# Block products for 16 of the 22 k tiles of the first FFN's down product

## Chip, cores and metric

The kernel runs on one core of a Trainium2 chip. The metric is the device time of one execution in microseconds. Three runs of the kernel before gave 1197.14, 1197.54 and 1198.35 us; the median is 1197.54.

## The reference

A transformer block on 512 tokens of width 1024 in fp32: an FFN, a mixer and a second FFN, each added to the residual x. The part that matters here is the first FFN.

```python
def swiglu(x, w_gu, w_down):
    g, u = jnp.split(x @ w_gu, 2, axis=-1)
    return (jax.nn.silu(g) * u) @ w_down
...
    for l in range(DEPTH):
        x = x + FFN_RES_WEIGHT * swiglu(rmsnorm(x, norm_ffn1_g[l]), ffn1_w_gu[l], ffn1_w_down[l])
        x = x + hybrid_mixer(rmsnorm(x, norm_mix_g[l]), w_in[l], ...)
        x = x + FFN_RES_WEIGHT * swiglu(rmsnorm(x, norm_ffn2_g[l]), ffn2_w_gu[l], ffn2_w_down[l])
```

FFN_RES_WEIGHT is 0.5 and the inner width D_FF is 2816, which is 22 k tiles of 128 (KF). The down product is 512 tokens x 2816 by 2816 x 1024.

## The kernel before

**Layout.** x and the hidden activations lie transposed: features on the 128 partitions, tokens along the free dimension. `hid` holds the 22 k tiles of the down product's input, each 128 x 512. X holds the residual, eight tiles of 128 x 512. Every fp32 factor is split into a rounded part h and a remainder l, and a product is three matmuls: h x h, h x l and l x h. For weights the two parts are the tiles `wh` (a cast on ScalarE, L335) and `wl` (a subtraction on VectorE, L336), in pools of three buffers each. For activations they are pairs of tiles `op`, 14 buffers in all.

**Plain k tiles.** One weight unit of 128 x 1024 is one k tile; `mm` multiplies it into eight PSUM banks, one for each of the eight output tiles d, with 3 x 8 = 24 matmuls of 512 columns (L363 to L365). [...]

**Sets.** A set computes 4 output tiles over 8 k tiles for all 512 tokens by seven block products in place of eight: k is halved into 4 + 4 tiles, the output columns into 256 + 256, the tokens into 256 + 256 (HW = 256), and sums of blocks are multiplied. The products are named m1, p2, q6, p5, q7, p4, p3. Each is 24 x matmul of 256 columns, written `Set.run` (L528), and is called a step below. The set's weights are four raw tiles a11, a12, a21, a22 of 128 x 1024. Their sums are made on the way: s3 = a11 + a21 on VectorE (L320), and a21 += a22, a11 += a21, a12 += a11 by accumulating transfers on POOL's queue (L310), each due before the product that uses it. m1, q6, q7 and p4 of a set accumulate in one bank, p2 in a second, p5 and p3 in a third. In the down product each product is added into X right after it (L741), so the bank must be read before the next of its products goes on in it.

**Operands.** The activation side of the seven products is an `Operands` object: seven parts, each a pair of `op` tiles. `make(p)` casts (ScalarE, L576) and subtracts (VectorE, L577); for p5, q6, q7 and p4 a sum in place on `hid` comes first (VectorE, L556 to L563). All sets over the same 8 k tiles share one such object, so one holds all 14 `op` buffers; a buffer comes free once the last set has used its part.

**Order.** `STEPS` lists units and products in the order in which TensorE takes them. `order` chains sets: the m1 and p2 of the next set stand among the last products of the present one. `Weights.issue` runs up to three steps ahead of TensorE: it loads raw tiles (SP's queue, L306, a pool `f` of 10 buffers), six steps ahead for a set, and converts them. A scheduler then sets each engine's order; every engine runs its queue in that order.

**The first FFN's down product** comes after a chain of nine up sets (the last is called the last up set below). The hidden tiles 8 to 19 are multiplied plainly (CHUNK = 8, TAIL1 = 2), and meanwhile the seven parts for tiles 0 to 7 are made. Two chained sets follow over tiles 0 to 7, one for each half of the output. Tiles 20 and 21 come last, plainly, since the last up set writes them; with them the next norm starts. The second FFN's down product (`last_down`) is another code path.

Of the kernel before, what the change touches and what calls it, by code (L numbers as in the profile page):

```python
# [17 lines left out]
D = 1024  # L18
KD = D // P
DFF = 2816  # L20
KF = DFF // P
# [19 lines left out]
TAIL = 4  # L41

TAIL1 = 2


def k_parts(kt):
# [3 lines left out]
def single(mat, kt, col):  # L50
    return [(mat, k0, nk, (col,), P) for k0, nk in k_parts(kt)]


def group(mat, kt, cols, slow=False):

    parts = [(0, 1), (1, 1)] if slow else [(0, 2)]
    parts += [(k0, 2) for k0 in range(2, kt, 2)]
    return [(mat, k0, nk, tuple(cols), P) for k0, nk in parts]
# [6 lines left out]
def full(mat, kt):  # L65
    return [(mat, k, 1, (0,), 1024) for k in range(kt)]
# [12 lines left out]
HW = 256  # L79


def order(firsts):


    seq = []
    n = len(firsts)
    for i, s in enumerate(firsts):
        if i == 0:
            seq += [(s, "m1"), (s, "p2")]
        seq += [(s, "q6"), (s, "p5"), (s, "q7")]  # L90
        if i + 1 < n:
            t = firsts[i + 1]
            seq += [(t, "m1"), (s, "p4")]
            seq += [(t, "p2"), (s, "p3")] if i + 2 < n else [(s, "p3")]
        else:
            seq += [(s, "p2"), (s, "p4"), (s, "p3")]
    return seq
# [6 lines left out]
PLAN = []  # L104
# [4 lines left out]
def units(us):  # L109
    for u in us:  # L110
        STEPS.append((len(PLAN), None))
        PLAN.append(u)


def sets(mat, pairs):
    firsts = []
    for cols in pairs:
        firsts.append(len(PLAN))
        PLAN.extend((mat, 4 * j, 4, (c,), HW) for c in cols for j in range(2))
    STEPS.extend(order(firsts))  # L120


# [7 lines left out]
CHUNK = 8  # L130
# [4 lines left out]
def last_plan(down):  # L135
    us = full(down, KF)
    units(us[CHUNK : KF - TAIL])
    firsts = []
    for s in range(2):
        firsts.append(len(PLAN))  # L140
        PLAN.extend((down, 4 * j + 2 * s, 2, (512 * i,), 512) for i in range(2) for j in range(2))
    CHUNK_STEP.update({(s, p): len(STEPS) + 2 * i + s for i, p in enumerate(CHUNK_ORDER)
                       for s in range(2)})
    STEPS.extend((n, p) for p in CHUNK_ORDER for n in firsts)
    units(us[KF - TAIL :])


def ffn_plan(up, down, plain, slow):

    units(group(up, KD, (0, DFF, P, DFF + P), slow))  # L150
    for f in range(2, plain):
        units(single(up, KD, f * P))
        units(single(up, KD, DFF + f * P))
    sets(up, [(s * HW, DFF + s * HW) for s in range(plain // 2, KF // 2)])
    if slow:
        us = full(down, KF)
        units(us[CHUNK : KF - TAIL1])
        sets(down, [(2 * s * HW, (2 * s + 1) * HW) for s in range(D // (2 * HW))])
        units(us[KF - TAIL1 :])
    else:  # L160
        last_plan(down)
    ENDS.append(len(STEPS))


def mixer_plan():
    units(group("w_in", KD, (QO, KO, QO + P, KO + P)))
    units(wide("w_in", KD, VO))
    for h in (2, 3):
        units(single("w_in", KD, QO + h * P))
        units(single("w_in", KD, KO + h * P))  # L170
    units(wide("w_in", KD, VO + 512))
    base = {"ga": GA, "gb": GB, "cb": CB, "r": RO}
    sets("w_in", [(CC + i * HW, CU + i * HW) if n == "conv" else
                  (base[n] + 2 * i * HW, base[n] + (2 * i + 1) * HW) for n, i in MSETS])
    for d in range(KD):
        units(single("w_out_conv", KD, d * P))
    for d in range(KD):
        units(single("w_out_gla", KD, d * P))
    units(group("w_o", KD, (0, P, 2 * P, 3 * P)))
    for d in range(4, KD):  # L180
        units(single("w_o", KD, d * P))
    ENDS.append(len(STEPS))
# [13 lines left out]
def block_kernel(ctx: ExitStack, tc: tile.TileContext, xT, vecs, gf, gup, wgl, wts, out):  # L196
# [5 lines left out]
    keep = ctx.enter_context(tc.tile_pool(name="keep", bufs=1))  # L202
    ps = ctx.enter_context(tc.tile_pool(name="ps", bufs=6, space=bass.MemoryType.PSUM))
# [14 lines left out]
    def tile_of(pool, shape, dtype=F32):  # L218
        cnt[0] += 1
        return pools[pool].tile(shape, dtype, tag=pool, name=f"{pool}{cnt[0]}")  # L220
# [141 lines left out]
    def mm3(o, wh, wl, ah, al, first, last):  # L362
        nc.tensor.matmul(o, wh, ah, start=first, stop=False)  # L363
        nc.tensor.matmul(o, wh, al, start=False, stop=False)  # L364
        nc.tensor.matmul(o, wl, ah, start=False, stop=last)  # L365
# [171 lines left out]
    class Operands:  # L537
# [29 lines left out]
        def make(self, p):  # L567
            if p in self.parts:
                return
            i = self.ORDER.index(p)  # L570
            if i > 0:
                self.make(self.ORDER[i - 1])
            v = self.sum(p)
            h, l = (tile_of("op", [P, 1024], F32R) for _ in range(2))
            hv, lv = (t.rearrange("p (k t) -> p k t", t=HW) for t in (h, l))
            nc.scalar.copy(hv, v)  # L576
            nc.vector.tensor_tensor(out=lv, in0=v, in1=hv.bitcast(F32), op=ALU.subtract)  # L577
            self.parts[p] = (h, l)
# [4 lines left out]
    def run_sets(make, ahead=2, hooks={}):  # L583


        at = W.taken
        seq = []
        while STEPS[at + len(seq)][1] is not None:
            seq.append(STEPS[at + len(seq)])
        sets = {n: None for n, _ in seq}  # L590
        number = {n: i for i, n in enumerate(sets)}
        for n, i in number.items():
            sets[n] = make(i)
        for i, (n, p) in enumerate(seq):
            for n_, p_ in seq[i : i + ahead + 1]:
                sets[n_].group.make(p_)
            sets[n].run(p)
            for f in hooks.get((number[n], p), ()):
                f()


    def ffn(up, down, norm, nxt, plain, at):
# [9 lines left out]
        hid = tile_of("hid", [P, KF, S])  # L612
# [69 lines left out]
        def pair(t):  # L682
            return t.rearrange("p (e t) -> p e t", t=HW)
# [3 lines left out]
        def split_hid(k):  # L687

            h, l = (tile_of("op", [P, 2, S], F32R) for _ in range(2))
            t = hid[:, k : k + 2]  # L690
            nc.scalar.copy(h, t)
            nc.vector.tensor_tensor(out=l, in0=t, in1=h.bitcast(F32), op=ALU.subtract)
            return h, l

        us = full(down, KF)
# [3 lines left out]
        def banks():  # L699
            return [AUX(), AUX()] + [MM() for _ in range(KD - 2)]  # L700

        def mm(d, k, w, hl):
            c = slice(d * P, (d + 1) * P)
            mm3(o[d], w[0][:, c], w[1][:, c], hl[0][:, k % 2], hl[1][:, k % 2],
                k in (CHUNK, KF - TAIL1), k in (KF - TAIL1 - 1, KF - 1))

        def add_half(d):
            nc.vector.scalar_tensor_tensor(out=x[d], in0=o[d], scalar=0.5, in1=x[d],
                                           op0=ALU.mult, op1=ALU.add)


        ho = Operands(lambda j, l: hid[:, 4 * j : 4 * j + 4, l * HW : (l + 1) * HW])
        o = banks()
        hls = {k: split_hid(k) for k in (CHUNK, CHUNK + 2)}
        more = [4, 6, 8, 10, "m1", "p2", "p5", "q6", "q7", "p3"]
        for k in range(CHUNK, KF - TAIL1):
            w = W.take(us[k])
            for d in range(KD):
                mm(d, k, w, hls[k - k % 2])
            if more:  # L720
                n = more.pop(0)
                if isinstance(n, int):
                    hls[CHUNK + n] = split_hid(CHUNK + n)
                else:
                    ho.make(n)
        for d in range(KD):
            add_half(d)
        ho.make("p4")

        X = XS[-1]  # L730

# [4 lines left out]
        def down_set(i):  # L736
            def done(s, p):
                for l, a, by in uses[p]:
                    xt = X[:, 4 * i + 2 * a : 4 * i + 2 * a + 2, l * HW : (l + 1) * HW]
                    bank = s.bank[{"p2": "a", "p5": "c", "p3": "c"}.get(p, "b")]  # L740
                    nc.vector.scalar_tensor_tensor(out=xt, in0=pair(bank), scalar=by, in1=xt,  # L741
                                                   op0=ALU.mult, op1=ALU.add)

            return Set(ho, done, keep=())

        run_sets(down_set)
        o = banks()
        w = [W.take(u) for u in us[KF - TAIL1 :]]
        hl = split_hid(KF - TAIL1)
        for d in range(KD):  # L750
            for i in range(TAIL1):
                mm(d, KF - TAIL1 + i, w[i], hl)
            add_half(d)
            nxt.add(d)
# [696 lines left out]
```

## Time and the profile before

| what | value |
|---|---|
| median of three runs | 1197.54 us (1197.14 to 1198.35) |
| profiled execution | its span, first to last instruction, is 1196.1 us; the page gives no other time for it, so its own device time is only known as about that of the runs, 1.4 us above the span at their median |
| mean granted TensorE clock | 0.998 |
| busy | PE 99%, PE weight load 92%, VectorE 69%, ScalarE 49%, POOL 8% |
| twelve plain down tiles | 232.20 to 297.51 us |
| two down sets | 297.51 to 337.82 us |

In the page's rows a group is: line, engine, operation, output <- input, count, busy time, mean duration, idle time ahead of it and what ended that. PE is matmuls, PEld weight loads, DVE VectorE, ACT ScalarE, POOL GpSimd and its queue, SP the queue of plain loads. A row of the windows gives each engine's busy time in a stretch and the count of its instructions, then the granted clock (1.00 is full) and what the transfers did. A row of the timeline gives start and duration.

### The profile page before, as it was taken

The page shows a single profiled execution, that of the slowest core. Times are in us where ns is not written, and L with a number is a line of the kernel's source. Part 1 is how long each engine was busy: PE and PEld are TensorE (multiplying, and loading weights), DVE is VectorE, ACT ScalarE, POOL GpSimd, SP SyncE. Part 2 cuts the span into 40 slices and gives each one's busy share as a digit, 9 for nine tenths or more (in the row PEclk, how much of TensorE's full clock was granted, in tenths as well). Part 3 has the DMA queues.
Part 4 walks back from the last instruction along what each step waited for, and adds up shares of the span by engine and source line. Part 5 has one row for each costly group of instructions (what it writes and reads, how often), then busy time and mean ns, then how long its engine had stood idle before and what let it go on. Part 6 is the DMA issues. An engine that isn't in the chain of part 4 may idle for free.

```text
span 1196.1 us, 19145 instructions
## 1 busy us (share of the span) xinstructions
PE 1188.1 (99%) x7858; PEld 1095.6 (92%) x7858; DVE 830.7 (69%) x997; ACT 587.3 (49%) x730; POOL 101.2 (8%) x137
## 2 busy tenths in 40 slices
PE   9999999999999999999999999999999999999997
PEld 8899999988988889999999998888889999998886
DVE  7976566844787765858678686555597656675685
ACT  6564444622354465646454574324355455562353
POOL 0011111000110001011011100100001111100100
PEclk9999999999999999999999999999999999999999
DMA  9377777533473225767767766613338777763431
GB/s 346 87 207 187 180 184 187 176 101 80 104 270 106 88 66 146 201 183 188 191 179 175 190 185 211 203 48 141 120 74 209 167 188 173 186 180 108 93 95 70
DMA packets 57607, 187.65 MB, mean 157 GB/s; under 512 B 6480, under 2 KB 10704, under 8 KB 57520
## 3 DMA queue, kind: packets, MB, share of 16 engines
q1 hardware_dynamic: 36912, 124.27, 29.5%
q0 software_dynamic: 15968, 57.68, 26.1%
q10 hardware_dynamic: 4640, 4.49, 1.2%
q8 instruction: 61, 1.00, 0.3%
q14 instruction: 26, 0.21, 0.1%
HBM read 124.55 MB, written 8.39 MB: 111 GB/s over the span
## 4 chain that ended last, share of the span: by engine, by line
PE 99%; ACT 0%; DVE 0%; issue 0%; POOL 0%; POOLq 0%
PE mm L528 54%; PE mm L387 7%; PE mm L363 6%; PE mm L365 6%; PE mm L364 6%; PE mm L829 3%; PE mm L779 2%; PE mm L780 2%; PE mm L778 2%; PE mm L405 1%; PE mm L406 1%; PE mm L404 1%; PE aux L1120 1%; PE aux L363 1%; PE aux L364 1%; PE aux L780 1%
## 5 line engine op out<-in xcount | busy, mean ns | idle before, releaser
L528 PE MATMUL mm<-op,wh 128*128 128x256 f32 x3584 | 648.0, 283 | 0.0
L335 ACT CAST wh<-f 128x1024 fp32r<-128x1024 f32 (+1 forms) x319 | 333.4, 1046 | 467.3 <-PE mm L528 235.3
L528 PEld LDWEIGHTS mm<-op,wh 128*128 128x128 f32 x3584 | 558.9, 192 | 1.0
L336 DVE TENSOR_TENSOR wl<-f,wh 128x1024 fp32r<-128x1024 f32 (+1 forms) x319 | 387.6, 1218 | 203.8 <-ACT wh L335 199.0
L528 PE MATMUL mm<-op,wl 128*128 128x256 f32 x1792 | 507.3, 283 | 0.0
L528 PEld LDWEIGHTS mm<-op,wl 128*128 128x128 f32 x1792 | 343.3, 192 | 0.3 <-DVE wl L336 0.2
L310 POOL DMA_DIRECT2D f<-f x102 | 88.2, 864 | 932.8 <-DVE wl L336 481.0
L363 PE MATMUL mm<-op,wh 128*128 128x512 f32 x340 | 132.7, 390 | 0.0
L365 PE MATMUL mm<-op,wl 128*128 128x512 f32 x340 | 132.5, 390 | 0.0
L364 PE MATMUL mm<-op,wh 128*128 128x512 f32 x340 | 132.3, 389 | 0.0
L365 PEld LDWEIGHTS mm<-op,wl 128*128 128x128 f32 x340 | 63.8, 188 | 13.4
L364 PEld LDWEIGHTS mm<-op,wh 128*128 128x128 f32 x340 | 63.8, 188 | 13.1
L363 PEld LDWEIGHTS mm<-op,wh 128*128 128x128 f32 x340 | 63.8, 188 | 13.1
L387 PE MATMUL mm<-op,wh 128*128 128x512 f32 x256 | 64.2, 393 | 0.0
L387 PEld LDWEIGHTS mm<-op,wh 128*128 128x128 f32 x256 | 48.5, 190 | 10.3
L533 ACT COPY tp<-mm 128x512 f32<-128x512 f32 x90 | 52.3, 581 | 0.0
L576 ACT CAST op<-hid 128x1024 fp32r<-128x1024 f32 x28 | 29.4, 1050 | 37.4 <-PE aux L779 20.7
L577 DVE TENSOR_TENSOR op<-hid,op 128x1024 fp32r<-128x1024 f32 x28 | 34.2, 1221 | 18.5 <-ACT op L576 18.5
L320 DVE TENSOR_TENSOR f<-f,f 128x1024 f32<-128x1024 f32 x34 | 41.6, 1223 | 0.9
L829 PE MATMUL mm<-wh,op 128*128 128x512 f32 x112 | 34.6, 389 | 0.0
L387 PE MATMUL mm<-op,wl 128*128 128x512 f32 x128 | 34.2, 389 | 0.0
L387 PEld LDWEIGHTS mm<-op,wl 128*128 128x128 f32 x128 | 24.0, 188 | 5.0
(253 smaller groups left out, 1136.6 us busy)
## 6 DMA issues: line engine op xcount, KB each, us to landing
f<-wts SPq DMA_DIRECT2D x219, 512.0 KB, 4.1
f<-f POOLq DMA_DIRECT2D x102, 512.0 KB, 4.8
X<-xT SPq DMA_DIRECT2D x8, 256.0 KB, 5.2
xs<-X POOLq DMA_DIRECT2D x8, 256.0 KB, 6.3
ga<-tp ACTq DMA_DIRECT2D x8, 256.0 KB, 4.0
gb<-tp ACTq DMA_DIRECT2D x8, 256.0 KB, 4.9
tp<-ga SPq DMA_DIRECT2D x8, 256.0 KB, 6.1
tp<-gb SPq DMA_DIRECT2D x8, 256.0 KB, 2.8
```

The source lines that it names most:

```text
L310: nc.gpsimd.dma_start(out_, a, accum_op=ALU.add)
L320: nc.vector.tensor_tensor(out=s3, in0=a11, in1=a21, op=ALU.add)
L335: nc.scalar.copy(h[:, :w], raw[:, :w])
L336: nc.vector.tensor_tensor(out=l[:, :w], in0=raw[:, :w], in1=h[:, :w].bitcast(F32), op=ALU.subtract)
L363: nc.tensor.matmul(o, wh, ah, start=first, stop=False)
L364: nc.tensor.matmul(o, wh, al, start=False, stop=False)
L365: nc.tensor.matmul(o, wl, ah, start=False, stop=last)
L387: nc.tensor.matmul(o[c], w[:, s : s + P], a[k], start=k == 0 and j == 0, stop=k == kt - 1 and j == 2)
L528: nc.tensor.matmul(to, ww[:, s], aa[:, t], start=fresh and k == 0 and e == 0 and j == 0, stop=k == 3 and j == 2, skip_group_check=True)
L533: nc.scalar.copy(v, o)
L780: nc.tensor.matmul(o[t][e], b, wh, start=False, stop=k in (KF - TAIL - 1, KF - 1))
L829: nc.tensor.matmul(to, aa[:, c], ww, start=fresh and k == 0 and n == 0, stop=k == 3 and n == 2, skip_group_check=True)
```

## The change

Tiles 0 to 3 (FILL1 = 4) are multiplied plainly, and tiles 4 to 19 by four chained sets: two over tiles 4 to 11, then two over tiles 12 to 19. Tiles 20 and 21 stay plain. There are now two `Operands`, one for each group of 8 tiles; the second takes over the `op` buffers of the first part by part. The first four parts are made beside the four plain tiles, the other three and all seven of the second object in hooks after products of the sets.

```diff
+FILL1 = 4
...
-def sets(mat, pairs):
+def sets(mat, pairs, bases=(0,)):
     firsts = []
-    for cols in pairs:
-        firsts.append(len(PLAN))
-        PLAN.extend((mat, 4 * j, 4, (c,), HW) for c in cols for j in range(2))
+    for base in bases:
+        for cols in pairs:
+            firsts.append(len(PLAN))
+            PLAN.extend((mat, base + 4 * j, 4, (c,), HW) for c in cols for j in range(2))
     STEPS.extend(order(firsts))
...
         us = full(down, KF)
-        units(us[CHUNK : KF - TAIL1])
-        sets(down, [(2 * s * HW, (2 * s + 1) * HW) for s in range(D // (2 * HW))])
+        units(us[:FILL1])
+        sets(down, [(2 * s * HW, (2 * s + 1) * HW) for s in range(D // (2 * HW))],
+             range(FILL1, KF - TAIL1, CHUNK))
         units(us[KF - TAIL1 :])
...
-                k in (CHUNK, KF - TAIL1), k in (KF - TAIL1 - 1, KF - 1))
+                k in (0, KF - TAIL1), k in (FILL1 - 1, KF - 1))
...
-        ho = Operands(lambda j, l: hid[:, 4 * j : 4 * j + 4, l * HW : (l + 1) * HW])
+        def operands(f):
+            return Operands(lambda j, l: hid[:, f + 4 * j : f + 4 * j + 4, l * HW : (l + 1) * HW])
+
+        ho = [operands(f) for f in range(FILL1, KF - TAIL1, CHUNK)]
         o = banks()
-        hls = {k: split_hid(k) for k in (CHUNK, CHUNK + 2)}
-        more = [4, 6, 8, 10, "m1", "p2", "p5", "q6", "q7", "p3"]
-        for k in range(CHUNK, KF - TAIL1):
+        hls = {0: split_hid(0), 2: split_hid(2)}
+        more = ["m1", "p2", "p5", "q6"]
+        for k in range(FILL1):
             w = W.take(us[k])
             for d in range(KD):
                 mm(d, k, w, hls[k - k % 2])
-            if more:
-                n = more.pop(0)
-                if isinstance(n, int):
-                    hls[CHUNK + n] = split_hid(CHUNK + n)
-                else:
-                    ho.make(n)
+            ho[0].make(more.pop(0))
         for d in range(KD):
             add_half(d)
-        ho.make("p4")
...
-                    xt = X[:, 4 * i + 2 * a : 4 * i + 2 * a + 2, l * HW : (l + 1) * HW]
+                    d = 4 * (i % 2) + 2 * a
+                    xt = X[:, d : d + 2, l * HW : (l + 1) * HW]
...
-            return Set(ho, done, keep=())
-
-        run_sets(down_set)
+            return Set(ho[i // 2], done, keep=())
+
+        makes = [(0, "q7"), (0, "p3"), (0, "p4")] + [(1, p) for p in Operands.ORDER]
+
+        def make():
+            c, p = makes.pop(0)
+            ho[c].make(p)
+
+        run_sets(down_set, hooks={(i, p): [make] for i, ps in
+                                  ((0, ("m1", "q6", "q7")), (1, ("m1", "q6", "p5", "q7", "p4")),
+                                   (2, ("q6", "q7"))) for p in ps})
```

Two places of the built order matter. The first is VectorE inside the down sets. Before, from the first set's q7 on, it has only the weights' remainder wl and the addition into X in turn (line numbers of the kernel before):

```order
L336 TENSOR_TENSOR wl424_3100<-f393_2856,wh423_3099 128x1024
L741 SCALAR_TENSOR_TENSOR X_88<-mm416_3036,X_88 128x2x256
L336 TENSOR_TENSOR wl427_3130<-f402_2925,wh426_3129 128x1024
L741 SCALAR_TENSOR_TENSOR X_88<-mm425_3128,X_88 128x2x256
L336 TENSOR_TENSOR wl429_3160<-f379_2755,wh428_3159 128x1024
L741 SCALAR_TENSOR_TENSOR X_88<-mm416_3036,X_88 128x2x256
```

Now, from the second set's p4 on, ending with the wl of the third set's q6 (wl442; f are raw weights, op and hid the activations; three lines further down in the file, so L339 is L336, L580 is L577, L323 is L320, L742 is L741, L561 and L564 the sums on hid):

```order
L339 TENSOR_TENSOR wl429_3144<-f365_2656,wh428_3143 128x1024
L561 SCALAR_TENSOR_TENSOR hid55_353<-hid55_353 128x4x256
L742 SCALAR_TENSOR_TENSOR X_88<-mm402_2940,X_88 128x2x256
L339 TENSOR_TENSOR wl434_3179<-f397_2905,wh433_3178 128x1024
L580 TENSOR_TENSOR op431_3174<-hid55_353,op430_3173 128x1024
L742 SCALAR_TENSOR_TENSOR X_88<-mm432_3177,X_88 128x2x256
L339 TENSOR_TENSOR wl436_3209<-f363_2652,wh435_3208 128x1024
L564 TENSOR_TENSOR hid55_353<-hid55_353 128x4x256
L742 SCALAR_TENSOR_TENSOR X_88<-mm402_2940,X_88 128x2x256
L323 TENSOR_TENSOR f440_3243<-f424_3135,f426_3139 128x1024
L580 TENSOR_TENSOR op438_3239<-hid55_353,op437_3238 128x1024
L339 TENSOR_TENSOR wl442_3247<-f396_2903,wh441_3246 128x1024
```

What moved: between two additions into X stands one wide operation before, and now two or three, since the second object's sums and subtractions come in.

The second place is SP's queue of loads at the end of the up sets. Before, the first plain tile (f318) is followed by the plain tiles one by one; the first down set's four (f376 to f379) come after ten more loads:

```order
L306 DMA f280_2052<-wts 128x1024
L306 DMA f318_2398<-wts 128x1024
L306 DMA f333_2524<-wts 128x1024
L306 DMA f334_2526<-wts 128x1024
L306 DMA f335_2528<-wts 128x1024
```

Now the first set's four (f325 to f328) stand ahead of plain tiles 1 to 3 (f337 to f339), and the second set's four (f362 to f365) follow at once:

```order
L309 DMA f280_2052<-wts 128x1024
L309 DMA f318_2398<-wts 128x1024
L309 DMA f325_2460<-wts 128x1024
L309 DMA f326_2462<-wts 128x1024
L309 DMA f327_2464<-wts 128x1024
L309 DMA f328_2466<-wts 128x1024
L309 DMA f337_2532<-wts 128x1024
L309 DMA f338_2534<-wts 128x1024
L309 DMA f339_2536<-wts 128x1024
L309 DMA f362_2650<-wts 128x1024
L309 DMA f363_2652<-wts 128x1024
L309 DMA f364_2654<-wts 128x1024
```

What moved: the plain tiles 1 to 3 are no longer next after tile 0. They take the buffers of the last up set's a21, s3 and a22; the second set's tiles f362 to f365 take those of its a12 and of plain tiles 0 to 2.

## Prediction, on record before the changed kernel was run

> **What bounds the kernel now.** I read the page's busy shares first.
>
> ```profile
> span 1196.1 us, 19145 instructions
> ...
> PE 1188.1 (99%) x7858; PEld 1095.6 (92%) x7858; DVE 830.7 (69%) x997; ACT 587.3 (49%) x730; POOL 101.2 (8%) x137
> ...
> PEclk9999999999999999999999999999999999999999
> ```
>
> TensorE is busy for 99% of the span at the full clock, so only two things move the time: how much matmul work there is, and whether a gap opens in it. An average over the span doesn't say what the changed stage does, so next comes the chain that ended last, around the first FFN's down product, and the busy times of three stretches: the last four sets of the up product, the twelve plain k tiles, the two down sets.
>
> ```profile
> 232.20 0.23 PE aux L363
> ...
> 297.51 40.31 PE mm L528 x336
> 337.82 0.23 PE aux L363
> ...
> core 0: us, PE busy (x) PEld busy (x) DVE busy (x) ACT busy (x) POOL busy (x), PEclk, DMA share, GB/s
> 151.52:232.20 80.68, 80.68 (x674) 80.68 (x673) 56.04 (x58) 44.73 (x54) 7.76 (x9) 1.00 0.70 184
> 232.20:297.51 65.31, 65.31 (x291) 54.06 (x290) 34.19 (x33) 19.04 (x20) 3.07 (x4) 1.00 0.35 98
> 297.51:337.82 40.31, 40.31 (x337) 40.31 (x337) 29.08 (x32) 16.38 (x16) 3.82 (x6) 1.00 0.46 124
> ```
>
> The reader is to see that TensorE has no gap in any of the three (busy time equals the length of the window), and that four chained sets, the form that the change asks for, already run so in the up product. VectorE has the least room there: 56.04 of 80.68 us.
>
> **What is removed and added.** Twelve plain tiles take 297.51 - 232.20 = 65.31 us, 5.44 each, or 226.8 ns for each of a tile's 24 matmuls of 512 columns. Two sets take 40.31 us for 336 matmuls of 256 columns: 120.0 ns each, 20.16 a set, 2.88 a block product ("step" below). Eight plain tiles go: 8 x 5.44 = 43.5. Two sets come: 40.3. If TensorE stays without a gap the sum is -3.2 us. There is one change from plain tiles to sets and one back, as before, so nothing is added for those. Block products save an eighth of the columns streamed; what is left of the eighth here is 3.2 of 43.5, about a fourteenth, since two 256-column matmuls (240.0 ns) cost more than one of 512 (226.8).
>
> [...]
>
> **What has to hide under TensorE.** For each step ScalarE rounds the weight tile (wh), VectorE forms the remainder (wl), and VectorE adds the product into X (L741). The changed kernel adds the second chain's operands: by the code ten of the fourteen parts of both chains are made inside the sets, each a cast on ScalarE and a subtraction on VectorE, and six need a sum on VectorE first (the built order takes the earliest of these ahead into the plain tiles). ScalarE, at 16.38 of 40.31 us, gets ten casts of 1.05 over 80.6 us: free. VectorE is the question. These are its rows in the present down sets, and a stretch without waiting some 90 us earlier.
>
> ```profile
> 314.70 1.05 ACT L335 CAST wh<-f 128x1024 fp32r<-128x1024 f32 x1 [1.83 <-PE mm L528]
> ...
> 315.78 1.23 DVE L336 TENSOR_TENSOR wl<-f,wh 128x1024 fp32r<-128x1024 f32 x1 [0.27 <-ACT wh L335]
> ...
> 226.32 1.23 DVE L336 TENSOR_TENSOR wl<-f,wh 128x1024 fp32r<-128x1024 f32 x1
> 227.46 0.68 DVE L660 TENSOR_TENSOR tp<-mm,tp 128x512 f32<-128x512 f32 x1
> 228.06 1.22 DVE L336 TENSOR_TENSOR wl<-f,wh 128x1024 fp32r<-128x1024 f32 x1
> 229.19 1.22 DVE L692 TENSOR_TENSOR op<-hid,op 128x1024 fp32r<-128x1024 f32 x1
> 230.33 0.69 DVE L669 SCALAR_TENSOR_TENSOR hid<-mm,tp 128x512 f32<-128x512 f32 x1
> 230.93 1.21 DVE L336 TENSOR_TENSOR wl<-f,wh 128x1024 fp32r<-128x1024 f32 x1
> ```
>
> Queued back to back, VectorE starts a 1024-wide operation every 1.14 us (229.19 to 230.33) and a 512-wide one every 0.60 (227.46 to 228.06, 230.33 to 230.93), though each row is 1.22 or 0.69 long. The spare time is read from the first two rows. Weight buffers are three deep, so the cast at 314.70 starts when step 5 of the two sets ends (297.51 + 6 x 2.88 = 314.79) and serves step 8, which begins at 297.51 + 8 x 2.88 = 320.55. Its wl ends at 315.78 + 1.23 = 317.01: 3.5 us to spare. A VectorE that lags by more than that stops TensorE.
>
> In the order of the changed kernel the fullest stretch runs from the wl of the first set's p3 (step 8) to just ahead of the wl of the third set's q6 (step 16). In it stand 17 wide operations (seven other wl, the p3 one, four subtractions for m1's successors p2, p5, q6 and q7, three sums, two of the sums s3) and 8 additions into X: 17 x 1.14 + 8 x 0.60 = 24.2 us, while TensorE takes 8 x 2.88 = 23.0. The lag grows by 1.1, on top of 1.1 from the m1 subtraction just ahead of the stretch. Of the 3.5 us, 1.2 are left at that wl. After it the queue thins (a step's own work is 1.14 + 0.60 = 1.7 of 2.88 us) and the lag goes. The second limit is the bank: q7 of the third set goes on in the bank of its q6, which VectorE must have read within the one step between them. Behind the tight wl stand four wide operations counting itself and two narrow ones (5.8 us) and then that read, so it starts 0.5 us after q6 ends, at 0.69 long, with 2.88 allowed: 1.7 to spare. I take nothing for the stall. From above I bound it by charging the 25 operations their full row times, 17 x 1.22 + 8 x 0.69 = 26.3: the lag is then 3.3 + 1.2 against 3.5, a stall of 1.0, and perhaps as much again from waits between the cast of a part and its subtraction: 2.0. Below nothing is excluded, since TensorE has no gap to give back. I go by the spacings, because the stretch from 227.46 is the same mixture of operations.
>
> **The plain stage.** It shrinks from 65.3 to 21.8 us. Between the wl of its first tile (begun at 228.06 in the rows above) and the wl of the first set's m1 the new order has 12 wide and 3 narrow operations on VectorE, 12 x 1.14 + 3 x 0.60 = 15.5 us; that wl is due at 232.20 + 21.8 = 254.0. The buffer it needs is free once plain tile 1 is done, at 243.1. No stall.
>
> **The loads.** The weight bytes are the same; the two new sets add six accumulating transfers on POOL's queue. What moves is who gets the free buffers: the first set's four tiles are now fetched ahead of plain tiles 1 to 3, which take buffers of the last up set, and the first set's s3 now stands on VectorE just ahead of that set's last wl. Around that wl the trace of before has
>
> ```profile
> 220.36 0.86 POOL L310 DMA_DIRECT2D f<-f  x1 [16.42 <-DVE wl L336]
> ...
> 225.23 2.18 ACT L335 CAST wh<-f 128x1024 fp32r<-128x1024 f32 x2 [0.22 <-DMA f<-f]
> ...
> f<-wts SPq DMA_DIRECT2D x219, 512.0 KB, 4.1
> f<-f POOLq DMA_DIRECT2D x102, 512.0 KB, 4.8
> ```
>
> The cast at 225.23 is that of the last up set's p3; it waited 0.2 us for the accumulation a12 += a11, issued at 220.36 and landed 4.8 later. Its wl, at 226.32 in the rows above, ends at 227.6; its step begins at 232.20 - 2.88 = 229.3. Of these 1.8 us the new s3 takes 1.1 at most, so 0.6 stay. The buffers of plain tiles 1 to 3 are free once that set's p5, q7 and p4 are converted, the last before 225.2; fetched then they land 4.1 later, about 229.3, and the earliest of them is needed at 232.20 + 5.44 = 237.6, cast and wl (2.3) included by 231.6. The second set's tiles stand behind them on SP's queue; their s3 has until the first set's m1, at 254.0. Nothing is charged.
>
> The sum: -3.2 us. The profiled span of 1196.1 becomes 1192.9; between that span and the median of 1197.54 lie 1.4 us that the change doesn't touch. Forecast: 1197.54 - 3.2 = 1194.3. About 0.2%, 2.4 us, is what a measurement of this kernel can tell from no change, so a stall of 0.8 us is enough to lose the sign.
>
> **Rivals.** *VectorE becomes the bound of the sets.* For it: the 1.2 us left at the third set's q6, a stretch with hardly an idle moment, and VectorE is in order, so a subtraction that waits for ScalarE's cast holds the wl behind it. Against it: the stretch from 227.46, and a TensorE stop gives VectorE the same time back, so it is paid once. It costs 0.8 to 2.0 us, giving 1195.1 to 1196.3, which reads as no change. It decides once the 25 operations take over 25.4 us.
>
> *The crowded entry, on the slower side.* Between about 217 and 240 seven loads and three accumulations come close together, and a late one blocks queues that run in order. Where ten loads were issued in 15 us, at the mixer's start, and where accumulations ran in this stage, landing took (least, median, most):
>
> ```profile
> L306 SPq DMA_DIRECT2D f<-wts x10: 327/424/631, 330.5 to 343.8; - x10
> ...
> DMA to landing us min/median/max: 3.3/5.2/12.1
> ...
> L310 POOL DMA_DIRECT2D f<-f x8: 862/862/883, 203.1 to 325.9; - x8
> ...
> DMA to landing us min/median/max: 4.5/4.7/6.3
> ```
>
> At 12.1 us for the accumulation of 220.36 the cast of the last up set's p3 starts at 232.5, its wl ends 2.3 later at 234.8, 5.4 after it is due. The second set's first tile takes that a12's buffer, so it lands at about 234.8 + 12.1 = 246.9; the s3 that needs it, two more operations and the first set's m1 wl follow on VectorE, to about 251.5, and POOL's a11 += a21 follows that: ready for use at 251.5 + 0.9 + 12.1 + 2.3 = 266.8, where the first set's q6 is due at 232.2 + 5.4 + 21.8 + 5.8 = 265.2. That is 1.6 more, 7.0 in all: 1197.5 - 3.2 + 7.0 = 1201.3. It decides from a landing of about 6.6 us (4.8 and the 1.8 of spare), less by the s3's 1.1; the accumulations' worst here is 6.3 and their median 4.7, so it needs the worst row to become the rule, and it needs a landing near 10 before the time is over that of before. [...]
>
> *The saving isn't there.* If 256-column products in a longer chain ran 1% slower, 0.8 us would go; the up product's four sets (80.68 us, 20.17 each) speak against it.
>
> **How the numbers follow.** Forecast 0.72; VectorE's lag, with the third rival, 0.18; the crowded entry and other blockages of an in-order queue 0.10. So faster 0.72, same 0.18, slower 0.10. The range starts 0.8 below the forecast, at 1193.5 (the three runs before spread from 0.4 below their median to 0.8 above), and ends at 1196.3, where VectorE's lag ends; the crowded entry is left out.
>
> **What would show it.** Right: four plain tiles in 21.8 us, 672 products in 80.6 without a gap, VectorE with almost no idle time for some 37 us in the middle, and the wl of the third set's q6 ending about 1 us ahead of its step. Wrong: a matmul of that q6 or of the next q7 that waits for wl or for an addition into X (the first rival), a cast that waits long for a transfer at the last up set's p3 or the first set's q6, with a gap on TensorE behind it (the second), or spacings other than 120.0 and 226.8 ns (the third).

## The result, and the profile after

The changed kernel takes 1195.88 us at the median (1194.28 to 1197.08, 20 runs), the kernel before 1197.86 on the same chip (1196.95 to 1198.67, 20 runs). The ratio is 0.9984, 95% interval 0.9978 to 0.9990: 2.0 us faster (1.2 to 2.6), where 3.2 was forecast. The sign and the range held; 1.2 us of the gain are missing.

The page of the changed kernel:

```profile
span 1193.6 us, 19497 instructions
...
PE 1184.4 (99%) x8002; PEld 1098.9 (92%) x8002; DVE 855.4 (72%) x1026; ACT 596.6 (50%) x739; POOL 106.3 (9%) x143
```

Its chain of waits around the stage (start, length, what):

```profile
232.19 0.23 PE aux L366
...
253.98 80.63 PE mm L531 x672
...
345.52 11.11 PE mm L390 x49
```

Its busy times in two stretches, the four plain tiles and the four down sets:

```profile
232.20:253.98 21.78, 21.78 (x98) 18.02 (x98) 20.05 (x22) 8.91 (x10) 2.59 (x3) 1.00 0.55 131
253.98:334.61 80.63, 80.63 (x673) 80.63 (x673) 68.47 (x73) 37.65 (x37) 8.60 (x11) 1.00 0.59 151
```

The stage is what was forecast: four plain tiles in 21.78 us, 672 products in 80.63 without a gap. The mixer's first products, the last row of the chain above, stand in the chain of the kernel before as

```profile
348.73 11.11 PE mm L387 x49
```

so 3.21 us are gained there. Now VectorE around the third set's q6, in the timeline of the changed kernel:

```profile
296.47 1.22 DVE L580 TENSOR_TENSOR op<-hid,op 128x1024 fp32r<-128x1024 f32 x1
297.60 1.22 DVE L339 TENSOR_TENSOR wl<-f,wh 128x1024 fp32r<-128x1024 f32 x1
298.74 0.69 DVE L742 SCALAR_TENSOR_TENSOR X<-mm,X 128x512 f32<-128x512 f32 x1
```

The tight wl ends at 298.82; its step begins at 253.98 + 16 x 2.88 = 300.06. The 1.2 us of spare that the walk gave are there.

What is lost is lost behind the stage. TensorE's waits over the whole program of the changed kernel (total, times, longest) have, beside one of 0.5 us at 5.6 us while the program starts, a row that the kernel before lacks:

```profile
PE mm L531 <- DVE wl L339: 0.4, 2, 0.2
```

One of the two is at the first up set of the second FFN (FFN2). ScalarE and TensorE there, in the timeline:

```profile
888.14 1.05 ACT L338 CAST wh<-f 128x1024 fp32r<-128x1024 f32 x1 [5.83 <-DMA f<-f]
...
893.11 0.39 PE L531 MATMUL mm<-op,wl 128*128 128x256 f32 x1 [0.16 <-DVE wl L339]
```

The same cast in the kernel before:

```profile
889.91 1.06 ACT L335 CAST wh<-f 128x1024 fp32r<-128x1024 f32 x1 [4.38 <-PE mm L364]
```

Before, ScalarE waited for a weight buffer that TensorE frees; now it waits for the accumulating transfer a11 += a21. The first set has the order m1, p2, q6, so this sum has only two steps. In the kernel before, the transfer's own rows (issue, and time to landing) are

```profile
L310 POOL DMA_DIRECT2D f<-f x1: 877/877/877, 885.1 to 885.1; - x1
...
DMA to landing us min/median/max: 4.5/4.5/4.5
```

and in the changed kernel

```profile
L313 POOL DMA_DIRECT2D f<-f x1: 877/877/877, 881.9 to 881.9; - x1
...
DMA to landing us min/median/max: 6.2/6.2/6.2
```

It lands in 6.2 us in place of 4.5, and TensorE stalls by 0.43 us there (what the starts of its matmuls, some 893 us into the span, lie apart beyond 120.0 ns).

A second loss lies at the very end. The work behind the last matmul is the same in both kernels, but the span ends 7.54 us after that matmul's start, and 7.23 in the kernel before. POOL's last two semaphore instructions, in the closing sequence of the program, start at these times (changed kernel first; counts, durations in ns, first and last start):

```profile
L1455 POOLq EVENT_SEMAPHORE  x2: 17/17/17, 1193.1 to 1193.5; - x2
```

```profile
L1446 POOLq EVENT_SEMAPHORE  x2: 17/17/17, 1195.9 to 1196.0; - x2
```

There are 0.35 us between them, and 0.06 in the kernel before. All ten traces of kernels with the change have 7.52 to 7.55 us behind the last matmul (in `p5_later`, below, the pause comes one instruction earlier), the four without it 7.23 to 7.25. The time outside the span grows too: the 20 timed executions of the changed kernel are 1.74 to 3.58 us longer than their spans, 2.03 on average. The kernel before, in 70 executions on three other chips, is 1.66 to 1.78 us longer, 1.72 on average; the 1.4 us given ahead of the prediction came from two different executions. Behind the last instruction all ten traces with the change have an instruction fetch of 8 KB that begins 0.5 to 0.6 us after the span, and none of the four without it has one. That fetches cause these two terms is not shown.

### The profile page after: what moved, and what is told of

It reads as the page before. It is cut to its first block, busy times and chain, and to the rows that moved or that the text cites. A ratio compares the mean times of both kernels' runs of the same rounds, so it can differ in the third digit from the quotient of the medians.

```text
span 1193.6 us, 19497 instructions
## 1 busy us (share of the span) xinstructions
PE 1184.4 (99%) x8002; PEld 1098.9 (92%) x8002; DVE 855.4 (72%) x1026; ACT 596.6 (50%) x739; POOL 106.3 (9%) x143
## 4 chain that ended last, share of the span: by engine, by line
PE 98%; ACT 0%; DVE 0%; issue 0%; DMA 0%; ACTq 0%
PE mm L531 57%; PE mm L390 7%; PE mm L366 6%; PE mm L368 6%; PE mm L367 6%; PE mm L838 3%; PE mm L789 2%; PE mm L787 2%; PE mm L788 2%; PE mm L407 1%; PE mm L409 1%; PE mm L408 1%; PE aux L1129 1%; PE aux L789 1%; PE aux L787 1%; PE aux L788 1%
## 5 line engine op out<-in xcount | busy, mean ns | idle before, releaser
L531 PE MATMUL mm<-op,wh 128*128 128x256 f32 x3808 | 688.5, 283 | 0.0
L531 PEld LDWEIGHTS mm<-op,wh 128*128 128x128 f32 x3808 | 593.8, 192 | 1.0
L338 ACT CAST wh<-f 128x1024 fp32r<-128x1024 f32 (+1 forms) x325 | 339.5, 1046 | 458.0 <-PE mm L531 242.8
L531 PE MATMUL mm<-op,wl 128*128 128x256 f32 x1904 | 539.1, 283 | 0.4 <-DVE wl L339 0.4
L339 DVE TENSOR_TENSOR wl<-f,wh 128x1024 fp32r<-128x1024 f32 (+1 forms) x325 | 395.1, 1218 | 179.3 <-ACT wh L338 174.5
L531 PEld LDWEIGHTS mm<-op,wl 128*128 128x128 f32 x1904 | 364.8, 192 | 0.9 <-DVE wl L339 0.8
L366 PE MATMUL mm<-op,wh 128*128 128x512 f32 x292 | 114.0, 390 | 0.0
L368 PE MATMUL mm<-op,wl 128*128 128x512 f32 x292 | 113.8, 390 | 0.0
L367 PE MATMUL mm<-op,wh 128*128 128x512 f32 x292 | 113.6, 389 | 0.0
L368 PEld LDWEIGHTS mm<-op,wl 128*128 128x128 f32 x292 | 54.8, 188 | 11.5
L367 PEld LDWEIGHTS mm<-op,wh 128*128 128x128 f32 x292 | 54.8, 188 | 11.3
L366 PEld LDWEIGHTS mm<-op,wh 128*128 128x128 f32 x292 | 54.8, 188 | 11.2
L390 PE MATMUL mm<-op,wh 128*128 128x512 f32 x256 | 63.7, 390 | 0.5 <-DVE op L441 0.5
L390 PEld LDWEIGHTS mm<-op,wh 128*128 128x128 f32 x256 | 48.0, 188 | 10.9 <-ACT acc L450 0.7
L580 DVE TENSOR_TENSOR op<-hid,op 128x1024 fp32r<-128x1024 f32 x35 | 42.7, 1221 | 16.1 <-ACT op L579 16.0
L579 ACT CAST op<-hid 128x1024 fp32r<-128x1024 f32 x35 | 36.6, 1048 | 32.0 <-PE aux L788 20.7
L323 DVE TENSOR_TENSOR f<-f,f 128x1024 f32<-128x1024 f32 x36 | 44.0, 1223 | 1.9 <-DMA f<-f 1.1
L390 PE MATMUL mm<-op,wl 128*128 128x512 f32 x128 | 34.4, 390 | 0.0
L390 PEld LDWEIGHTS mm<-op,wl 128*128 128x128 f32 x128 | 23.9, 188 | 5.3 <-DVE wl L339 0.3
```

The costliest lines, as they stand in the source:

```text
L323: nc.vector.tensor_tensor(out=s3, in0=a11, in1=a21, op=ALU.add)
L338: nc.scalar.copy(h[:, :w], raw[:, :w])
L339: nc.vector.tensor_tensor(out=l[:, :w], in0=raw[:, :w], in1=h[:, :w].bitcast(F32), op=ALU.subtract)
L390: nc.tensor.matmul(o[c], w[:, s : s + P], a[k], start=k == 0 and j == 0, stop=k == kt - 1 and j == 2)
L531: nc.tensor.matmul(to, ww[:, s], aa[:, t], start=fresh and k == 0 and e == 0 and j == 0, stop=k == 3 and j == 2, skip_group_check=True)
```

## Experiments

**Theory.** The stage gave its 3.2 us; the 1.2 were lost where q6 of an up chain's first set waits for its accumulating transfer. What delays that is an instruction fetch: the queues' rows of the changed kernel have

```profile
q8 instruction: 62, 1.02, 0.3%
```

62 packets of 16 KB. From the start of the first to that of the last, TensorE starts 15530 matmuls and weight loads, 254.6 for each of the 61 intervals; before, with 61 packets, 15286, 254.8 for each of 60. So one packet seems to bring about 255 TensorE instructions, an estimate from these counts (single intervals have 210 to 298). The change adds 288 of them, 16004 for 15716, and the later fetches fall at other places in the work: the one nearest this transfer begins 3.96 us after its issue in place of 5.90. **Rivals.** The loss lies in the down stage in executions that weren't profiled (VectorE), or the transfer is late for another reason.

### The changed kernel again, and the later q6

`after_again` is the changed kernel itself.

> The changed kernel, unchanged, as the mark for the three kernels beside it. All theories: 1.2 to 2.6 us under the kernel before. The theory (the stage gained its 3.2 us whole, and some of it is lost again behind it, where the first up set of FFN2 waits for a late accumulating load) expects in the trace no gap on TensorE in the down stage and one of about 0.4 us ahead of the third product of that first up set, near 893; its rival (the one profile is an accident, and the loss lies in the down stage in the other executions) expects gaps between 254 and 335 in some trace.

Measured: 1196.30 us, 0.9985 of the kernel before (0.9976 to 0.9994). The stage is again 80.63 us without a gap. The transfer landed in 6.7 us, and the waits in its timeline have grown:

```profile
889.11 1.05 ACT L338 CAST wh<-f 128x1024 fp32r<-128x1024 f32 x1 [6.33 <-DMA f<-f]
...
894.08 0.38 PE L531 MATMUL mm<-op,wl 128*128 128x256 f32 x1 [0.34 <-DVE wl L339]
```

Its stall near 893 is 0.92 us. The first rival has nothing for it.

```diff
+        if i == 0 and later:          # later: the up sets of FFN2 only
+            seq += [(s, "p5"), (s, "q6"), (s, "q7")]
+        else:
+            seq += [(s, "q6"), (s, "p5"), (s, "q7")]
```

> The changed kernel with the first up set of FFN2 in the order m1, p2, p5, q6 in place of m1, p2, q6, p5, so that the accumulating load that q6 needs has one product (2.88 us) more. Theory (the missing 1.2 us was lost at that wait, in the profiled execution and more of it in the timed ones): no gap near 890, and 0.4 to 1.2 us less than the changed kernel of the same chip, 2.6 to 3.2 us less than the kernel before. Rival (the loss is elsewhere, in the down stage or at the end): the gap near 890 goes, and the time stays within 0.2 us of the changed kernel.

Measured: 1194.72 us, 0.9977 (0.9967 to 0.9986), 2.8 under the kernel before. In this execution the transfer was as late as in `after_again`, 6.8 us, and in its chain of waits TensorE runs on:

```profile
888.98 16.09 PE mm L535 x133
```

One step more for the transfer takes the stall away: the wait is a place of the loss. By the ratios that is worth 1.0 us over `after_again`, though the two intervals overlap. Why the transfer is late this doesn't tell.

### The phase of the fetches

`phase_late` has 16 TensorE instructions less, at the start, for the same time:

```diff
-    ones = front.tile([P, P], F32, tag="ones", name="ones")
+    ones = front.tile([P, 213], F32, tag="ones", name="ones")
-    for i in range(10):
-        nc.tensor.matmul(warm[:, :P], ones, ones, start=True, stop=True)
+    for i in range(6):
+        nc.tensor.matmul(warm[:, :213], ones[:, :P], ones, start=True, stop=True)
```

> The changed kernel with six warm-up products of 213 columns in place of ten of 128 at the start: as long, but 16 TensorE instructions less, so that every 16 KB instruction fetch of TensorE (one in some 15 us in a set) falls about 1 us later against the work. Theory (a fetch that arrives 1 to 4 us after an accumulating load was issued holds it up by about 1.4 us; the change's 144 more products shifted the fetch onto the one that FFN2's first up set waits for): that load lands in under 5.5 us in place of 6.2, the gap near 893 is gone or under 0.1 us, and the time is 0.4 to 1.2 us under the changed kernel. Rival (the landing of 6.2 us comes from the other loads in flight, which are the same here): it lands in about 6 us again, the gap stays at 0.3 to 0.5 us, and the time is the changed kernel's within 0.2 us.

Measured: 1194.65 us (1194.31 to 1195.01), 0.9974 (0.9963 to 0.9984), 3.1 us under the kernel before and 1.3 under `after_again`, a little more than expected. By the means 1.05 us of that lie in the span and 0.24 outside it, where all eight executions have 1.73 to 1.83 us. The transfer lands in 4.6 us (its own rows), and ScalarE's cast waits for TensorE again (timeline):

```profile
L314 POOL DMA_DIRECT2D f<-f x1: 877/877/877, 881.9 to 881.9; - x1
...
DMA to landing us min/median/max: 4.6/4.6/4.6
```

```profile
886.78 1.05 ACT L339 CAST wh<-f 128x1024 fp32r<-128x1024 f32 x1 [4.39 <-PE mm L368]
```

The opposite test gives the kernel before 36 instructions more:

```diff
+            if k == CHUNK + 4 and d < 6:
+                ...  # each of the three matmuls as two of 256 columns
```

> The kernel before, with 18 products of 512 columns in one of its plain down tiles of FFN1 issued as two of 256 each: 36 TensorE instructions more, which cost 18 x (2 x 120.0 - 226.8) = 0.24 us and let every later instruction fetch fall about 2 us earlier against the work. Theory of the fetch: the load that FFN2's first up set waits for, 4.5 us in the kernel before, takes about 6 us, a gap of about 0.4 us appears ahead of q6 there, and the time is 0.6 to 1.4 us over the kernel before. Rival (the fetch does nothing): it lands in 4.5 us, no gap, and 0.2 to 0.3 us over the kernel before.

Measured: 1198.84 us, 1.0004 (0.9995 to 1.0013): can't be told from the kernel before. In its trace the added matmuls cost 0.25 us, as worked out. But the fetch came only 1.2 us earlier, 4.69 us after the transfer's issue, which landed in 5.1 and cost nothing: in this execution the expected stall didn't come. The eleven times fall in two groups, five from 1197.23 to 1198.06 us, with the profiled one, and six from 1198.84 to 1199.47; the kernel before beside it has 1197.07 to 1198.93. The six may be executions with the stall, but no trace of one was kept. The packets show how two executions can differ there. The transfers' view of `after_again` from 887.0 to 888.3 us, when the fetch had just begun:

```profile
core 0 of [0], span 1194.5 us
...
DMA packets 1, 0.00 MB, mean 0 GB/s; under 512 B 1, under 2 KB 1, under 8 KB 1
...
q0 software_dynamic: 1, 0.00, 0.1%
```

The same view of `lag2` (below), whose work is the same there, from 886.96, likewise just behind the fetch's start, to 888.3:

```profile
core 0 of [0], span 1193.6 us
...
DMA packets 0, 0.00 MB, mean 0 GB/s; under 512 B 0, under 2 KB 0, under 8 KB 0
```

The transfer ends with sixteen packets of 4 bytes. Fifteen of the sixteen had come by 886.53 in `after_again`; then the fetch of 0.90 us began, 4.60 us after the issue, and the sixteenth came at 887.85, behind it. In `lag2` the sixteenth came at 886.93, just ahead of the fetch. That the two meet on one DMA engine is not shown: the records name no engine. The same in the packet records of all fourteen executions:

| kernel | fetch begins after issue | 15 small packets done / last | landing | stall at q6 |
|---|---|---|---|---|
| before | 5.90 us | 889.26 / 889.29 | 4.5 | 0 |
| phase_before | 4.69 | 889.59 / 890.08 | 5.1 | 0 |
| after | 3.96 | 886.07 / 887.56 | 6.2 | 0.43 |
| after_again | 4.60 | 886.53 / 887.85 | 6.7 | 0.92 |
| lag1 | 4.61 | 886.73 / 888.04 | 6.7 | 0.92 |
| lag2 | 4.61 | 886.50 / 886.93 | 5.2 | 0 |
| late | 4.60 | 886.02 / 886.44 | 5.2 | 0 |
| phase_late | 4.30 | 886.16 / 886.25 | 4.6 | 0 |
| p5_later | 4.73 | 886.55 / 888.04 | 6.8 | 0 (order) |
| warm_before | none in 8 us | 888.96 / 888.99 | 4.5 | 0 |
| lag4 | 4.60 | 890.06 / 890.48 | 5.2 | 0 |
| p5_before | 5.95 | 889.22 / 889.24 | 4.5 | 0 |
| p5_all | 4.03 | 886.34 / 887.90 | 6.2 | 0 (order) |
| both | 4.28 | 886.46 / 886.54 | 4.6 | 0 |

In the kernel before, the fetch comes when all is over, 5.90 us after the issue. In the kernels with the change it comes after 3.96 to 4.73 us, about when the last small packet does, and which of the two goes first differs between executions of the same work. In the six executions with landings of 5.1 or 5.2 us, or 4.6, the fetch begins within 4 ns of the start of the last 4-byte packet, so its start seems to go with that packet (read from these times; what ties them is not seen), and a shift by so many instructions doesn't shift it by their time. `phase_late` shows this too: its fetch begins 4.30 us after the issue, between the 3.96 and 4.60 of the two executions of the changed kernel, but behind the last packet. How far its request moved is not seen. Nor is it seen what keeps the last packet 0.4 to 0.5 us behind the others where the landing is 5.1 or 5.2.

The first FFN's (FFN1's) first up set has the same wait, near 56 us, ahead of the change. There the fetch begins 1.5 to 2.0 us after the issue in both kernels: landing 5.9 and a stall of 0.29 us before, 6.2 and 0.56 in `after`, 6.4 and 0.76 in `after_again`; 4.7 and none in `phase_late`. With the code ahead of it and the warm-up unchanged, this stall is 0.29, 0.79 and 0.07 us in `before`, `phase_before` and `p5_before`, and 0 to 0.82 in the seven traces of kernels with the change and the first order in FFN1: it differs between executions, and these traces don't show that the change made it larger.

### Is the warm-up, or the order, a gain by itself?

`warm_before` is the kernel before with the warm-up of `phase_late`; `p5_before` the kernel before with the order of `p5_later`.

> The kernel before with the warm-up of phase_late (six products of 213 columns in place of ten of 128). It gives the mark for what the change is worth when neither kernel's two waits meet a fetch. Theory: the fetch leaves the accumulating load that FFN1's first up set waits for (landing 5.9 us in the kernel before, 4.7 here), the stall near 56 goes, and the time is 0.1 to 0.5 us under the kernel before; phase_late, 3.1 under the kernel before on its chip, is then 2.6 to 3.2 under this. Rival (the other warm-up is a gain of about 1.1 us by itself, at the start, and says nothing of the fetches): 0.8 to 1.3 us under the kernel before.

Measured: 1197.48 us, 0.9999 (0.9990 to 1.0008). FFN1's transfer lands in 4.8 us and its stall is gone.

> The kernel before with the first up set of FFN2 in the order m1, p2, p5, q6. It shows whether that order is a gain by itself or only mends what the change lost. Theory (in the kernel before the instruction fetch comes 5.9 us after the accumulating load was issued, 1.4 us after it landed, so q6 doesn't wait): the time of the kernel before, within 0.3 us. Rival (the order is worth 0.8 us in any kernel, and p5_later's gain says nothing of the change): 0.6 us or more under the kernel before.

Measured: 1197.76 us, 1.0000 (0.9990 to 1.0009). At the medians they are 0.2 and 0.05 us under the kernel before (the intervals reach to 1.2), so neither shows a gain of its own like the 1.3 and 1.0 us that the ratios give them over `after_again`. With `warm_before` and `phase_late` the change can be weighed without either stall. From the first block product to the last matmul, by the starts in their timelines (`warm_before` first):

```profile
50.16 0.40 PE L529 MATMUL mm<-op,wh 128*128 128x256 f32 x2
...
1188.52 0.39 PE L781 MATMUL aux<-op,op 128*128 128x512 f32 x1
```

```profile
50.55 0.40 PE L532 MATMUL mm<-op,wh 128*128 128x256 f32 x2
...
1185.70 0.39 PE L790 MATMUL aux<-op,op 128*128 128x512 f32 x1
```

1138.36 and 1135.15 us: 3.21 apart, the forecast. The closing of the program takes 0.30 of that back (7.25 and 7.55 us behind the last matmul). The same distance is 1138.61 in the kernel before (0.25 over its clear twin, its stall of 0.29), 1136.08 in `after` (0.93 over; stalls 0.43 + 0.56) and 1136.75 in `after_again` (1.60 over; 0.92 + 0.76).

### The order in both FFNs, and both cures

> The changed kernel with the later q6 in the first up sets of both FFNs. FFN1's has the same wait: a gap of about 0.3 us near 57 stands in six of ten traces so far, of kernels with and without the change, where a fetch falls into its accumulating load and that lands in 5.9 to 6.4 us. Theory: no gap on TensorE near 57 and none near 890, whatever the loads take; 2.8 to 3.5 us under the kernel before, so 0 to 0.4 under p5_later. Rival (what is left has another cause): as p5_later, 0.9977 of the kernel before, with the gap near 57 or with another in its place.

Measured: 1195.64 us, 0.9982 (0.9974 to 0.9991). The gaps near 57 and 890 are gone, and the time is hardly under that of the changed kernel: the second half of the expectation failed. (Its count of earlier traces is too low as well: eight of the ten have the gap near 57, of 0.27 to 0.82 us.) In this trace the later q6 brings 0.40 us of small waits at 63 and 68 us (0.13 in FFN2, at 904), and another wait showed at 356, ahead of the mixer's `aux` products:

```profile
356.69 0.47 PE L982 MATMUL aux<-op,g 128*96 128x512 f32 x1 [0.17 <-DVE g L967]
```

> The same with the other warm-up (six products of 213 columns), which moves the fetch off both loads. Theory (either of the two is enough, so that together they bring no more): within 0.3 us of p5_all and of phase_late, 2.8 to 3.5 us under the kernel before. Rival (fetches also cost elsewhere, and the phase decides it): over 0.3 us under p5_all.

Measured: 1195.28 us, 0.9978 (0.9969 to 0.9987), 2.5 us under the kernel before at the medians, where 2.8 to 3.5 were expected. It is 0.36 under `p5_all`, just on the rival's side, and not better than `phase_late`. It has the small waits at 63, 68 and 904 too. The two cures don't add up; where the fetch is out of the way, the later q6 only costs in this trace: from the first block product to the last matmul it takes 1135.65 us, 0.50 over `phase_late`. `phase_late` has the lowest ratio, 0.9974, which can't be told from `p5_later`'s 0.9977.

### How near VectorE is

Dummy additions in the fullest stretch (n = 1, 2, 4; nothing reads them, and they write hidden tiles that are no longer needed), and the changed kernel without hooks:

```diff
+        def lag():                       # behind p3 of the first set
+            for i in range(n):
+                nc.vector.tensor_tensor(out=hid[:, 0:2], in0=X[:, 4:6], in1=X[:, 4:6], op=ALU.add)
```

> The changed kernel with one addition of 128x1024 more on VectorE, which nothing uses, behind the eighth product of the down stage, inside the stretch in which VectorE is never idle. Theory (the weight remainder of the third set's q6 ends 1.24 us ahead of its step, and nothing ahead of it is tighter): VectorE runs 1.14 us later from there on, the remainder ends about 0.1 us ahead, TensorE shows no gap over 0.2 us in the stage, and the stage is as long as without it. Rival (VectorE is already what bounds the stage, and its gaps only do not show): a gap of 1.1 us.

Measured: the four sets take 80.63 us again, without a gap. The tight wl ends 1.14 us ahead of its step, hardly nearer than without the addition (the next run shows why). Its one time, 1196.50 us, has the late transfer and its stall of 0.92 in it.

> The same with two such additions, 2.28 us. Theory: a gap of 1.0 to 1.3 us on TensorE, between step 8 and step 16 of the stage, and the end of the stage later by as much. Rival (the spare is larger than the walk gave, since VectorE's order is not what the products wait for): no gap.

Measured: no gap up to step 16, and 0.32 us of gaps at 312 us, step 20; not 1.0 to 1.3. The tight wl in its timeline:

```profile
298.75 1.22 DVE L339 TENSOR_TENSOR wl<-f,wh 128x1024 fp32r<-128x1024 f32 x1
299.89 1.22 DVE L580 TENSOR_TENSOR op<-hid,op 128x1024 fp32r<-128x1024 f32 x1
```

It ends at 299.97, 0.04 ahead of its step (253.93 + 46.08). The scheduler has put the subtraction that stood ahead of this wl behind it, as in `lag1`, so that two additions moved it by 1.2 and not by 2.3.

> The same with four, 4.56 us. Theory: gaps of 3.3 to 3.6 us in all. Rival (the spare is larger): under 2.3 us.

Measured: the stage 3.7 us longer, but not as expected. There is one gap, at 286 to 288 us, and slow matmuls behind it. The timeline, and then the busy times of three windows, in which the third number from the right is the granted clock:

```profile
288.14 0.39 PE L531 MATMUL mm<-op,wl 128*128 128x256 f32 x1 [1.95 <-DVE wl L339]
```

```profile
284.00:285.90 1.90, 1.90 (x18) 1.90 (x17) 1.90 (x3) 0.07 (x2) 0.00 (x0) 1.00 0.84 315
289.20:292.40 3.20, 3.20 (x18) 3.20 (x17) 3.20 (x4) 1.04 (x1) 0.04 (x1) 0.52 0.86 164
292.60:296.00 3.40, 3.40 (x30) 3.40 (x30) 3.40 (x5) 1.68 (x2) 0.00 (x0) 0.98 0.42 154
```

2.2 us of gap, and some 1.4 of matmuls that start every 213 ns in place of 120. By the gap alone the rival (under 2.3) would have it; the length agrees with the theory by accident.

> The changed kernel without the eleven hooks in the down sets: each right-hand operand is made when a product two steps ahead needs it, so that the second group's seven come in the first steps of the third set. Theory (the spread of the operands is what keeps VectorE under TensorE): a gap of 1 to 2 us in all on TensorE between steps 12 and 18, and the mixer as much later. Rival (the order of the operands does not matter, since VectorE has enough time in the stage as a whole, 78% of it): no gap.

Measured: no gap; the four sets take 80.63 us, as with the hooks (ten, not eleven). The expectation failed: the operands' order in the code matters little here. The likely reason, not tested, is that making one two steps ahead of its product spreads them too, and that the scheduler sorts what is left. Its one time is 1195.01 us; the transfer landed in 5.2 us.

## Why the prediction was right, and where not

- **The sum of the stage.** Right to the hundredth: 21.78 and 80.63 us, mixer 3.21 earlier, 3.21 between the two kernels without stalls. 226.8 and 120.0 ns held, so the rival that the saving isn't there is out.
- **VectorE's walk.** Right in its number, 1.24 us of spare for 1.2, and in its sign: VectorE waits for nothing from 272.3 to 311.0 us, 38.7 us for the 37 forecast. What it didn't have is that the scheduler re-sorts when there is more to do: two additions cost 0.3 where fixed queues would have lost about 1. So the stall of "0.8 to 2.0 us" had less behind it than 0.18 for that group suggests.
- **The loads at the entry.** No gap. The wl of the last up set's p3, begun at 228.02, ends at 229.24, when its step begins at 229.3: 0.1 of spare where 0.6 was worked out.
- **What lies behind the stage, and outside the span.** This is the step that failed. The sum let all later work move up by 3.2 us at no charge, and it took the time outside the span as something "that the change doesn't touch". Three terms were put at nothing. The wait at FFN2's first up set, 560 us behind the edit, is 0.43 us in `after`, 0.92 in `after_again` and `lag1`, and none in `lag2`, `lag4` and `late`: 0.38 on average over the six traces with the first order and warm-up. The closing of the program is 0.3 longer in all ten traces with the change. The time outside the span is 0.3 longer on average. As an estimate these are 1.0 of the 1.2 us that are missing (0.6 to 2.0 by the interval). "The loads ... Nothing is charged" looked at the down stage alone, though the row of the page that names the instruction queue was there, and the kernel before has a wait with no spare of the same form at 56 us. How often an execution without a profile stalls, and why the closing and the time outside the span grow, stays open.

## What to carry to other kernels

An edit that gains in its stage can lose some of it far behind. Here an instruction fetch 560 us on began 3.96 to 4.61 us after a transfer's issue in place of 5.90, and in three of the six traces with the first order and warm-up TensorE stalled there, by 0.43 to 0.92 us. So compare the waits of the whole program, its closing and the time outside the span, not only the waits of the stage. Look first for a transfer with two steps or less between issue and use, and give it a step more or move the fetch; here either cure brought back about a microsecond, and both together no more. Where a scheduler sorts the queues, spare time worked out from one order need not hold for another: here two additions of 1.14 us each cost 0.32.

## What the runs showed of the hardware

- A transfer of 512 KB and a 16 KB instruction fetch of 0.9 us beside it: in the five traces in which the last of the transfer's sixteen small packets came behind the fetch (`after`, `after_again`, `lag1`, `p5_later`, `p5_all`), the transfer landed in 6.2 to 6.8 us; in the nine in which that packet came ahead of the fetch (in `warm_before` no fetch came within 8 us), in 4.5 to 5.2. The landing came 0.32 us after the last small packet in `before`, 0.48 in `after` and 1.17 in `after_again`; what fills that time is not seen.
- In the one execution of `lag4` a gap of 2.1 us on TensorE was followed by 3.2 us at a granted clock of 0.52 (289.2 to 292.4 us), and the stage took 3.7 us longer. After the stall of 0.43 us in `after` the granted clock from 893 to 897 us was 1.00, and after the gaps of up to 0.6 us in `after_again` the chain of waits has 148 matmuls in 18.00 us, 122 ns each, where `lag4` has 213 ns at its clock of 0.52.
